# Multiplying the gates by the gelu straight out of PSUM in the dense expert loop

## The chip, the core and the metric

The kernel is one program on one core of a Trainium2 chip. It has five engines that run their own instruction streams in order: TensorE (PE, matrix products, results into PSUM banks), VectorE (DVE), ScalarE (ACT), GpSimd (POOL) and SyncE (SP, which here only issues transfers). The metric is the device time of one execution in microseconds. Three runs of the kernel before took 5031.38, 5035.41 and 5036.19 us; the median is 5035.41 us.

## The reference, cut to what matters

One layer of a hybrid backbone for 256 context tokens and 1024 sample tokens. The part that counts here is the last stage, PEER: 16384 experts of one neuron each, of which every token uses 16 in each of 8 heads.

```
idx  = top-16 experts of each head      # 128 of 16384 for a token
g    = softmax(scores of those)
act  = gelu(x . u_tab[idx])             # first layer
out  = sum over idx of (g * act) * v_tab[idx]   # second layer
```

The product `g * act` is what the change touches. A layer norm follows. Output: both token groups and the final states of a recurrence that runs earlier.

## The kernel before, in words

Two methods compute PEER side by side. The first 640 sample tokens (5 blocks of 128, `DB = 5`) go through all 16384 experts as dense matrix products, with a gate of zero where a token does not use an expert. The other 3 sample blocks and the context tokens are *gathered*: for each of a token's 128 experts a row of `u`, and later of `v`, is fetched by an indirect transfer issued on POOL, and DVE multiplies and adds it up, one instruction of 128x1024 for each row (`experts`, lines 1063 for `u` and 1072 for `v`). The vectors `h` and `y` of that sum live in PSUM, in a pool `pg` of one buffer.

The dense loop (`dense`, line 1133) runs over 32 steps `c` of 4 chunks of 128 experts each, `n = 4c + e`. For a chunk, `weighted(n)` gives the weights W, 128 experts x 640 tokens: gates `gt` (loaded from `d_GD`, two chunks to a tile) times the gelu of the first layer. For 72 of the 128 chunks (`EARLY`) the gelu was computed in an earlier stage and is loaded back from `d_AD` into a tile `a`; for the other 56 `first_layer` computes it here: two halves of 320 tokens, each 24 matmuls into one PSUM bank, which ACT turns into `a` by a gelu (line 1122). DVE multiplies `gt` by `a` (line 1160, 128x640). Then ACT copies W to `wh`, and DVE or POOL subtracts to get the rest `wl` (lines 205 and 206: every product is done as three products of rounded parts, so the tables `u` and `v` are split into `uh`, `ul`, `vh`, `vl` in the same way). The second layer multiplies W of the previous step by the table `v`: token block 0 adds up in two banks (`sums`) over the whole loop; blocks 1 to 4 take two banks each in every step, which DVE adds to `acc` (line 1146).

The dense loop's banks come from two pools of two buffers (`pa`, `pb`), taken in turn, so a product can begin when the bank of four products earlier is free. Before the change a first-layer bank is free after its gelu, a second-layer bank after its addition on DVE.

The order on each engine is made by a scheduler at build time, from its own model of times; gathered rows, dense additions and splits are mixed on DVE in that fixed order. A wait of one instruction holds up all behind it on that engine. At the end of a gathered block, `finish` (lines 1022 to 1035) norms and stores it, and the next block's `h` is loaded (line 1057) when the stored tile's buffer is free.

Of the kernel before, what the change touches and what calls it, by code (L numbers as in the profile page):

```python
# [11 lines left out]
F32 = mybir.dt.float32  # L12
# [4 lines left out]
AF = mybir.ActivationFunctionType  # L17
ALU = mybir.AluOpType
AX = mybir.AxisListType

P = 128
# [15 lines left out]
DB = 5  # L37
# [13 lines left out]
HALF = DB * P // 2  # L51
WSHARE = 0.5
GT = 64
# [48 lines left out]
def body(ctx, tc, A, O):  # L102
    nc = tc.nc
# [46 lines left out]
    def bank(s, banks=None):  # L150
        n = count["bank"] = count["bank"] + 1
        banks = banks or s.banks
        return banks[n % len(banks)].tile([P, 512], F32, tag="bank", name=f"bank{n}")

    def mm(out, terms, first=True, last=True):
        ops = []
        for l, r in terms:
            if len(l) == 1:
                ops.append((l[0], r[0]))
            else:  # L160
                ops += [(l[0], r[0]), (l[0], r[1]), (l[1], r[0])]
        for i, (l, r) in enumerate(ops):
            nc.tensor.matmul(out, l, r, start=(first and i == 0), stop=(last and i == len(ops) - 1))  # L163
# [33 lines left out]
    def elt(share):  # L197

        count["lo"] += 1
        n = count["lo"]  # L200
        return nc.gpsimd if int(n * share) != int((n - 1) * share) else nc.vector

    def split_into(hi, lo, src, eng):

        nc.scalar.activation(hi, src, AF.Copy)  # L205
        note(eng, eng.tensor_tensor(lo, src, hi.bitcast(F32), op=ALU.subtract))  # L206
# [14 lines left out]
    def sub(op, *idx):  # L221
        return tuple(o[idx] for o in op)
# [690 lines left out]
    def new_T(pool, s, nb):  # L913
        if s.native:
            return (pool.tile([P, KT, nb * P], F32, name="hT"),)
        return (pool.tile([P, KT, nb * P], F32R, name="hTh"), pool.tile([P, KT, nb * P], F32R, name="hTl"))
# [91 lines left out]
    def final_vectors(s, new):  # L1008
        vec = []
        for src in (mod_d[s.c:s.c + 1, 5 * D:6 * D], A["ln2_g"], A["ln2_b"]):  # L1010
            t = new()
            nc.sync.dma_start(t[:], src.to_broadcast([P, D]))
            vec.append(t)
        return vec
# [11 lines left out]
    def second_norm(s, b, y, out, pool, vec, eng):  # L1026
        rows = slice(b * P, (b + 1) * P)
        st = pool.tile([P, 2, 6], F32, tag="st", name="st", bufs=2)
        for i in range(2):
            nc.vector.bn_stats(st[:, i, :], y[:, i * 512:(i + 1) * 512])  # L1030
        sc, of = statistics(pool, st[:], EPS)
        nc.scalar.activation(y[:], y[:], AF.Identity, scale=sc, bias=of)
        nc.vector.tensor_tensor(y[:], y[:], vec[1][:], op=ALU.mult)
        eng.tensor_tensor(y[:], y[:], vec[2][:], op=ALU.add)
        nc.sync.dma_start(out[rows, :], y[:])
# [72 lines left out]
    def table(pool, src, tag, bufs, raws, eng):  # L1108

        r = pool.tile([P, D], F32, tag="raw" + tag, name="raw", bufs=raws)  # L1110
        nc.sync.dma_start(r[:], src)
        return split(pool, r[:], [P, D], tag, bufs=bufs, eng=eng)

    def first_layer(s, T, n, pool, bufs, share):

        U = table(pool, A["peer_uT"][n].rearrange("p k e -> p (k e)"), "u", bufs, 2, elt(share))
        a = pool.tile([P, DB * P], F32, tag="a", name="a", bufs=2)
        for t0 in range(0, DB * P, HALF):
            ts = slice(t0, t0 + HALF)
            ps = bank(s)  # L1120
            mm(ps[:, :HALF], [(sub(U, ALL, slice(k * P, (k + 1) * P)), sub(T, ALL, k, ts)) for k in range(KT)])
            nc.scalar.activation(a[:, ts], ps[:, :HALF], AF.Gelu_apprx_tanh)
        return a

    def dense(s, T, GD, AD, pool, accs, out):

        def spare():
            count["spare"] += 1
            return pool.tile([P, D], F32, tag=("uh", "uh", "uh", "ul", "ul", "ul", "rawu", "rawu", "rawv", "rawv")[count["spare"]], name="spare", bufs=2 if count["spare"] > 5 else 3)

        def second_layer(c, W, V, b):
            for h in range(2):
                cs = slice(h * 512, (h + 1) * 512)
                kept = b == 0
                ps = sums[h] if kept else bank(s)
                mm(ps[:], [(sub(W[e], ALL, slice(b * P, (b + 1) * P)), sub(V[e], ALL, cs)) for e in range(4)], c == 0 or not kept, c == 31 or not kept)
                if kept and c < 31:
                    continue
                if c == 0:
                    nc.scalar.activation(accs[b][:, cs], ps[:], AF.Copy)  # L1140
                elif c == 31:
                    t = pool.tile([P, 512], F32, tag="a", name="t", bufs=2)
                    nc.vector.tensor_tensor(t[:], ps[:], vec[0][:, cs], op=ALU.mult)
                    nc.vector.tensor_tensor(accs[b][:, cs], accs[b][:, cs], t[:], op=ALU.add)
                else:
                    nc.vector.tensor_tensor(accs[b][:, cs], accs[b][:, cs], ps[:], op=ALU.add)  # L1146

        pair = {}

        def weighted(n):  # L1150
            if n % 2 == 0:
                pair[0] = pool.tile([P, DB * P // GT, 2, GT], F32, tag="gt", name="gt", bufs=2)
                nc.sync.dma_start(pair[0][:], GD[:, :, n:n + 2, :].rearrange("c p j t -> p c j t"))
            gt = pair[0][:, :, n % 2, :]
            if n in EARLY:
                a = pool.tile([P, DB * P], F32, tag="a", name="a", bufs=2)
                nc.sync.dma_start(a[:], AD[EARLY.index(n)])
            else:
                a = first_layer(s, T, n, pool, 3, 0.5)
            nc.vector.tensor_tensor(gt, a[:].rearrange("p (c t) -> p c t", t=GT), gt, op=ALU.mult)  # L1160
            hi, lo = (pool.tile([P, DB * P], F32R, tag="w" + i, name="w" + i, bufs=6) for i in "hl")
            split_into(*(t[:].rearrange("p (c t) -> p c t", t=GT) for t in (hi, lo)), gt, elt(WSHARE))
            return hi, lo

        sums = [pc.tile([P, 512], F32, tag="bank", name=f"sums{h}") for h in range(2)]
        last, todo = None, []
        for c in range(33):
            W, V = [], []
            if c == 32:
                vec = final_vectors(s, spare)  # L1170
                for b in range(DB):
                    x = spare()
                    nc.sync.dma_start(x[:], s.X1[b * P:(b + 1) * P, :])
                    if b == 0:
                        accs[b] = spare()
                        nc.scalar.activation(accs[b][:], x[:], AF.Copy, scale=ALPHA)
                        continue
                    (nc.gpsimd if TP else nc.vector).tensor_tensor(accs[b][:], accs[b][:], vec[0][:], op=ALU.mult)
                    nc.vector.scalar_tensor_tensor(accs[b][:], x[:], ALPHA, accs[b][:], op0=ALU.mult, op1=ALU.add)
            for e in range(4):  # L1180
                if c < 32:
                    W.append(weighted(4 * c + e))
                if e < 2:
                    for b in todo[:3]:
                        second_layer(c - 1, *last, b)
                    todo = todo[3:]
                if c < 32 and e > 0:
                    for i in ((0,), (1, 2), (3,))[e - 1]:
                        V.append(table(pool, A["peer_v"].rearrange("(i j) d -> j i d", j=NK)[4 * c + i], "v", 4, 2, elt(0.5)))
            last, todo = (W, V), list(range(DB))  # L1190
        x = spare()
        nc.sync.dma_start(x[:], s.X1[s.nt - P:, :])
        for b in range(DB):
            second_norm(s, b, accs[b], out, pool, vec, nc.gpsimd if b < TB else nc.vector)
        return vec, x
# [37 lines left out]
    with tpool(SP, "tp") as fp:  # L1233
        T = new_T(fp, SP, SP.tt)
# [236 lines left out]
```

## Time and profile before

| | us |
|---|---|
| profiled execution | 5048.65 |
| its span | 5046.9 |
| median of three runs | 5035.41 |
| dense loop on PE, from its first second-layer product | 3577 to 4885 |
| after the dense loop | 4885 to 5047 |

PE is busy 4327.6 us (86%), DVE 4040.6 (80%), POOL 3176.4 (63%), ACT 1901.8 (38%) of the span. These are averages over stages with different limits; only the last 1470 us run the code that is changed. An instruction's time in the trace goes on until its result is written, so two in a row overlap a little: from the start of one to the start of the next is less than the time shown for one. The granted clock of TensorE stands as a share of its full speed.

### The profile page before, as it was taken

To read this page: it belongs to the slowest core of one execution; us is meant where nothing else is said; L and a number is where in the kernel's file an instruction comes from. 1 tells how busy PE (TensorE), PEld (TensorE's weight loads), DVE (VectorE), ACT (ScalarE), POOL (GpSimd) and SP (SyncE) were. 2 spreads that over 40 slices of the span, in tenths; PEclk is the share of its full clock that TensorE was granted. 3 is DMA by queue.
4 is the path that set the end of the run, shared out by engine and by line. 5 is a ranking of instruction groups with operands and counts; after the bars stand their busy time and mean duration, and the time that the engine had idled before them with its cause. 6 is when DMAs were issued, how large, how long until landed. Compare 5 with 4: busy or idle time off the path is not lost.

```text
span 5046.9 us, 67691 instructions
## 1 busy us (share of the span) xinstructions
PE 4327.6 (86%) x23707; PEld 3762.1 (75%) x23707; DVE 4040.6 (80%) x6725; ACT 1901.8 (38%) x2795; POOL 3176.4 (63%) x2297
## 2 busy tenths in 40 slices
PE   6888798899999679879798888889799999999970
PEld 4666687777777669857677888889688888888860
DVE  6778664989995786566759899887688989988898
ACT  4546333336664112221433765555222222222210
POOL 1456442478887665467665577778566676766775
PEclk8999899999999889989899999999899999999985
DMA  6676656798889853388786477788988999989987
GB/s 209 222 233 202 184 175 203 247 326 301 299 303 341 296 189 124 96 322 299 263 275 212 147 267 289 256 290 301 332 313 317 342 328 345 330 307 342 314 316 300
DMA packets 601089, 1357.25 MB, mean 269 GB/s; under 512 B 63230, under 2 KB 283079, under 8 KB 595116
## 3 DMA queue, kind: packets, MB, share of 16 engines
q1 hardware_dynamic: 404908, 658.69, 39.0%
q0 software_dynamic: 187776, 680.61, 37.6%
q10 hardware_dynamic: 8064, 13.64, 0.7%
q8 instruction: 186, 3.05, 0.2%
q14 instruction: 155, 1.27, 0.1%
HBM read 1182.81 MB, written 169.93 MB: 268 GB/s over the span
## 4 chain that ended last, share of the span: by engine, by line
PE 21%; DVE 17%; issue 8%; DMA 7%; POOL 4%; ACT 1%; SPq 0%; POOLq 0%; ACTq 0%; DVEq 0%
PE bank L163 16%; PE bank L172 3%; DVE row L1063 3%; DVE y L1072 2%; POOL row L1050 2%; DMA row<-in_peer_v,idxQ 2%; DVE hot L1094 2%; PE sums L163 2%; DMA row<-in_peer_v,idxP 1%; DVE gt L1160 1%; DMA row<-in_peer_u,idxQ 1%; DVE half L968 1%; DVE terms L972 1%; DVE S L932 1%; PE bank L1101 1%
## 5 line engine op out<-in xcount | busy, mean ns | idle before, releaser
L1072 DVE SCALAR_TENSOR_TENSOR y<-row,act,y 128x1024 f32<-128x1024 f32 x635 | 816.2, 1285 | 179.2 <-DMA row<-in_peer_v,idxP 109.4
L1063 DVE SCALAR_TENSOR_TENSOR row<-row,h 128x1024 f32<-128x1024 f32 x640 | 763.8, 1213 | 129.3 <-DMA row<-in_peer_u,idxP 69.9
L163 PE MATMUL bank<-hTh,ul 128*128 128x320 f32 x2048 | 642.9, 317 | 25.4 <-POOL ul L206 25.1
L163 PE MATMUL bank<-hTh,uh 128*128 128x320 f32 x2048 | 645.4, 315 | 11.7 <-ACT uh L205 11.7
L163 PE MATMUL bank<-hTl,uh 128*128 128x320 f32 x2048 | 645.7, 316 | 0.0
L1050 POOL DMA_INDIRECT row<-in_peer_u,idxQ x384 | 421.3, 1097 | 264.4 <-DVE row L1063 161.7
L206 POOL TENSOR_TENSOR wl<-wr,wh 128x1024 fp32r<-128x1024 f32 x148 | 363.9, 2460 | 333.7 <-ACT wh L205 311.9
L1050 POOL DMA_INDIRECT row<-in_peer_v,idxQ x384 | 416.2, 1084 | 246.8 <-DVE y L1072 163.8
L163 PEld LDWEIGHTS bank<-hTh,ul 128*128 128x128 f32 x2048 | 391.0, 192 | 33.9 <-POOL ul L206 33.7
L163 PE MATMUL bank<-vh,wh 128*128 128x512 f32 x1024 | 397.5, 393 | 17.8 <-DVE acc L1146 16.3
L163 PEld LDWEIGHTS bank<-hTh,uh 128*128 128x128 f32 x2048 | 394.2, 192 | 14.3 <-ACT uh L205 13.0
L163 PE MATMUL bank<-vl,wh 128*128 128x512 f32 x1024 | 400.3, 392 | 0.0
L163 PE MATMUL bank<-vh,wl 128*128 128x512 f32 x1024 | 395.7, 391 | 0.0
L163 PEld LDWEIGHTS bank<-hTl,uh 128*128 128x128 f32 x2048 | 393.4, 192 | 1.2
L1050 POOL DMA_INDIRECT row<-in_peer_u,idxP x256 | 276.3, 1079 | 143.6 <-DVE row L1063 83.6
L205 ACT ACTIVATE wh<-wr 128x1024 fp32r<-128x1024 f32 x176 | 186.0, 1059 | 442.8 <-issue 192.7
L1050 POOL DMA_INDIRECT row<-in_peer_v,idxP x256 | 279.9, 1093 | 92.5 <-issue 36.7
L1095 POOL TENSOR_TENSOR oa<-hot,tr 128x512 f32<-128x512 bf16 x160 | 220.2, 1386 | 85.9 <-DVE hot L1094 59.1
L205 ACT ACTIVATE wh<-gt 128x640 fp32r<-128x640 f32 x128 | 94.5, 740 | 466.0 <-DVE gt L1160 384.2
L206 POOL TENSOR_TENSOR ul<-raw,uh 128x1024 fp32r<-128x1024 f32 x100 | 245.6, 2456 | 27.6 <-ACT uh L205 24.3
L1098 ACT ACTIVATE ob<-hot 128x512 f32<-128x512 bf16 x160 | 181.3, 1136 | 184.7 <-DVE hot L1094 169.6
L1101 PE MATMUL bank<-ob,oa 128*128 128x128 f32 x1280 | 188.7, 294 | 66.1 <-POOL oa L1095 51.1
(455 smaller groups left out, 12697.9 us busy)
## 6 DMA issues: line engine op xcount, KB each, us to landing
raw<-in_peer_uT SPq DMA_DIRECT2D x128, 512.0 KB
raw<-in_peer_v SPq DMA_DIRECT2D x128, 512.0 KB
wr<-in_w_in SPq DMA_DIRECT2D x112, 512.0 KB
d_GD<-G SPq DMA_DIRECT2D x40, 1024.0 KB
gt<-d_GD SPq DMA_DIRECT2D x64, 640.0 KB
w<-in_w_ada SPq DMA_DIRECT2D x48, 512.0 KB
wr<-in_w_query SPq DMA_DIRECT2D x48, 512.0 KB
d_AD<-a SPq DMA_DIRECT2D x72, 320.0 KB
```

What stands on the lines that cost most here:

```text
L163: nc.tensor.matmul(out, l, r, start=(first and i == 0), stop=(last and i == len(ops) - 1))
L172: nc.tensor.matmul(out, a, b, start=(i + j == 0), stop=(i == KT - 1 and j == len(ops) - 1))
L205: nc.scalar.activation(hi, src, AF.Copy)
L206: note(eng, eng.tensor_tensor(lo, src, hi.bitcast(F32), op=ALU.subtract))
L932: nc.vector.match_replace(S2[:], v[:, g, 0:8], Sg, NEG)
L1050: i = nc.gpsimd.indirect_dma_start(out=t[:], out_offset=None, in_=A[tab], in_offset=bass.IndirectOffsetOnAxis(ap=idx[:, k:k + 1], axis=0))
L1063: nc.vector.scalar_tensor_tensor(t[:], t[:], 1.0, h[:], op0=ALU.mult, op1=ALU.mult, accum_out=act[:, k:k + 1])
L1072: nc.vector.scalar_tensor_tensor(y[:], t[:], act[:, k:k + 1], y[:], op0=ALU.mult, op1=ALU.add)
L1094: nc.vector.tensor_tensor(hot[:].rearrange("p k t q -> p k (t q)"), keys8[:], key[:, None, t0:t0 + 4, :].rearrange("p o t q -> p o (t q)") ...
L1095: note(nc.gpsimd, nc.gpsimd.tensor_tensor(oa[:], hot[:, :, :, 0].rearrange("p k t -> p t k"), tr[:, 2, t0:t0 + 4, None].to_broadcast([P, 4 ...
L1098: nc.scalar.activation(ob[:], hot[:, :, :, 1].rearrange("p k t -> p t k"), AF.Copy)
L1101: nc.tensor.matmul(ps[:, i * P:(i + 1) * P], oa[:, i, :], ob[:, i, :], start=True, stop=True)
```

## The change

For the 56 chunks whose first layer runs in the dense loop, the gelu is written back into the PSUM bank that it reads, and DVE multiplies `gt` by it from there, half by half: two instructions of 128x320 with one operand in PSUM, in place of one of 128x640 with both in SBUF. The tile `a` is no longer used for these chunks, only for the 72 that are loaded. The early stage calls `first_layer` without gates and is as before.

```diff
-    def first_layer(s, T, n, pool, bufs, share):
+    def first_layer(s, T, n, pool, bufs, share, gt=None):
         U = table(pool, A["peer_uT"][n].rearrange("p k e -> p (k e)"), "u", bufs, 2, elt(share))
-        a = pool.tile([P, DB * P], F32, tag="a", name="a", bufs=2)
+        if gt is None:
+            a = pool.tile([P, DB * P], F32, tag="a", name="a", bufs=2)
         for t0 in range(0, DB * P, HALF):
             ...
-            nc.scalar.activation(a[:, ts], ps[:, :HALF], AF.Gelu_apprx_tanh)
-        return a
+            if gt is None:
+                nc.scalar.activation(a[:, ts], ps[:, :HALF], AF.Gelu_apprx_tanh)
+            else:
+                nc.scalar.activation(ps[:, :HALF], ps[:, :HALF], AF.Gelu_apprx_tanh)
+                part = gt[:, t0 // GT:(t0 + HALF) // GT, :]
+                nc.vector.tensor_tensor(part, ps[:, :HALF].rearrange("p (c t) -> p c t", t=GT), part, op=ALU.mult)
+        return None if gt is not None else a
...
                 nc.sync.dma_start(a[:], AD[EARLY.index(n)])
+                nc.vector.tensor_tensor(gt, a[:].rearrange("p (c t) -> p c t", t=GT), gt, op=ALU.mult)
             else:
-                a = first_layer(s, T, n, pool, 3, 0.5)
-            nc.vector.tensor_tensor(gt, a[:].rearrange("p (c t) -> p c t", t=GT), gt, op=ALU.mult)
+                first_layer(s, T, n, pool, 3, 0.5, gt)
```

The change also shifts the order that the scheduler makes. Line 1160 becomes 1164 (loaded chunks) and 1128 (the new halves), line 1146 becomes 1152.

On DVE, where the last gathered block begins (its `h` is about to be loaded), before; `bank_36291` to `bank_36333` are the banks of token blocks 1 and 2 of one step:

```order
L1033 TENSOR_TENSOR r<-r,row 128x1024
L1160 TENSOR_TENSOR gt<-a,gt 128x10x64
L206 TENSOR_TENSOR vl<-raw,vh 128x1024
L1160 TENSOR_TENSOR gt<-a,gt 128x10x64 x2
L206 TENSOR_TENSOR wl<-gt,wh 128x640 x2
L1146 TENSOR_TENSOR acc_29995<-acc_29995,bank_36291 128x512
L1146 TENSOR_TENSOR acc_29995<-acc_29995,bank_36305 128x512
L1063 SCALAR_TENSOR_TENSOR row,act<-row,h 128x1024 x4
L1146 TENSOR_TENSOR acc_29996<-acc_29996,bank_36319 128x512
L1146 TENSOR_TENSOR acc_29996<-acc_29996,bank_36333 128x512
```

And the same place after the change:

```order
L1033 TENSOR_TENSOR r<-r,row 128x1024
L1128 TENSOR_TENSOR gt<-bank_36221,gt 128x5x64
L206 TENSOR_TENSOR vl<-raw,vh 128x1024
L206 TENSOR_TENSOR wl<-gt,wh 128x640 x2
L1063 SCALAR_TENSOR_TENSOR row,act<-row,h 128x1024 x4
L1152 TENSOR_TENSOR acc_29995<-acc_29995,bank_36291 128x512
L1152 TENSOR_TENSOR acc_29995<-acc_29995,bank_36305 128x512
L1063 SCALAR_TENSOR_TENSOR row,act<-row,h 128x1024
L1152 TENSOR_TENSOR acc_29996<-acc_29996,bank_36319 128x512
L1152 TENSOR_TENSOR acc_29996<-acc_29996,bank_36333 128x512
```

The first four gathered rows of the new block have moved ahead of the two additions of token block 1.

On DVE at the end of the dense loop, before; `acc_29998` is the last token block's sum, and `y` the gathered block's:

```order
L1072 SCALAR_TENSOR_TENSOR y<-row,act,y 128x1024
L1033 TENSOR_TENSOR acc_29998<-acc_29998,spare 128x1024
L1072 SCALAR_TENSOR_TENSOR y<-row,act,y 128x1024
L1034 TENSOR_TENSOR acc_29998<-acc_29998,spare 128x1024
L1072 SCALAR_TENSOR_TENSOR y<-row,act,y 128x1024 x76
L1022 TENSOR_TENSOR r<-y,spare 128x1024
```

And after the change:

```order
L1072 SCALAR_TENSOR_TENSOR y<-row,act,y 128x1024
L1033 TENSOR_TENSOR acc_29998<-acc_29998,spare 128x1024
L1072 SCALAR_TENSOR_TENSOR y<-row,act,y 128x1024
L1034 TENSOR_TENSOR acc_29998<-acc_29998,spare 128x1024
L1072 SCALAR_TENSOR_TENSOR y<-row,act,y 128x1024 x71
L1022 TENSOR_TENSOR r<-y,spare 128x1024
```

76 gathered rows stand behind the last dense instruction before, and 71 now. Counted from the addition that reads the last dense bank, there are 86 before and 80 now.

## Rows read from the trace of the kernel before

**Rows 1.** Stages: window, length, busy time by engine, clock, DMA share, GB/s.
```profile
core 0: us, PE busy (x) PEld busy (x) DVE busy (x) ACT busy (x) POOL busy (x), PEclk, DMA share, GB/s
3577.00:4885.00 1308.00, 1278.66 (x6503) 1116.36 (x6504) 1136.10 (x1298) 333.85 (x443) 882.12 (x646) 0.99 0.92 326
4885.00:5047.00 162.00, 5.58 (x24) 4.27 (x24) 144.91 (x144) 8.49 (x12) 95.59 (x90) 0.53 0.81 301
```

**Rows 2.** Timeline of DVE at the end: start, length, instruction, count.
```profile
4958.97 74.16 DVE L1072 SCALAR_TENSOR_TENSOR y<-row,act,y 128x1024 f32<-128x1024 f32 x56 [0.33 <-DVE y L1072]
```

**Rows 3.** Waits in the dense loop: us in total, times, longest.
```profile
ACT wh L205 <- DVE gt L1160: 369.1, 96, 10.9
DVE acc L1146 <- PE bank L163: 53.5, 58, 2.9
PE bank L163 <- DVE acc L1146: 16.3, 6, 6.6
```

**Rows 4.** Groups in the dense loop: busy us, mean ns; idle before, releasers.
```profile
L1160 DVE TENSOR_TENSOR gt<-a,gt 128x640 f32<-128x640 f32 x126 | 169.6, 1347 | 30.2 <-issue 19.0 <-ACT a L1122 4.9 <-DMA a<-d_AD 3.6
L1146 DVE TENSOR_TENSOR acc<-acc,bank 128x512 f32<-128x512 f32 x240 | 160.2, 684 | 54.9 <-PE bank L163 53.5 <-issue 0.7
```

**Rows 5.** Two lines by source: shortest, median, longest in ns.
```profile
L1160 DVE TENSOR_TENSOR gt<-a,gt x126: 811/821/5840, 3594.2 to 4867.0; 128x640 f32<-128x640 f32 x126
L1146 DVE TENSOR_TENSOR acc<-acc,bank x240: 672/684/692, 3646.6 to 4849.1; 128x512 f32<-128x512 f32 x120
```

**Rows 6.** Timeline of POOL and DVE around single instructions.
```profile
4401.20 2.40 POOL L206 TENSOR_TENSOR ul<-raw,uh 128x1024 fp32r<-128x1024 f32 x1 [0.33 <-issue]
4401.54 2.75 DVE L1160 TENSOR_TENSOR gt<-a,gt 128x640 f32<-128x640 f32 x1 [0.55 <-ACT a L1122]
4038.59 0.82 DVE L1160 TENSOR_TENSOR gt<-a,gt 128x640 f32<-128x640 f32 x1
4039.33 1.21 DVE L1063 SCALAR_TENSOR_TENSOR row<-row,h 128x1024 f32<-128x1024 f32 x1
4138.02 2.48 DVE L1146 TENSOR_TENSOR acc<-acc,bank 128x512 f32<-128x512 f32 x4
```

**Rows 7.** Timeline of PE: the products that followed the larger gaps.
```profile
3779.35 0.80 PE L163 MATMUL bank<-vh,wh 128*128 128x512 f32 x1 [3.78 <-DVE acc L1146]
4138.76 0.50 PE L163 MATMUL bank<-vh,wh 128*128 128x512 f32 x1 [2.37 <-DVE acc L1146]
4416.50 0.50 PE L163 MATMUL sums<-vh,wh 128*128 128x512 f32 x1 [1.78 <-issue]
4472.55 0.80 PE L163 MATMUL bank<-vh,wh 128*128 128x512 f32 x1 [6.60 <-DVE acc L1146]
4747.73 0.50 PE L163 MATMUL sums<-vh,wh 128*128 128x512 f32 x1 [1.51 <-ACT wh L205]
```

**Rows 8.** Stages again: just behind the gap at 3779.
```profile
3780.00:3790.00 10.00, 10.00 (x36) 8.07 (x35) 3.20 (x5) 1.03 (x1) 0.78 (x1) 0.78 0.80 269
```

**Rows 9.** Timeline of DVE, ACT and PE ahead of two gaps.
```profile
3753.50 3.16 DVE L1160 TENSOR_TENSOR gt<-a,gt 128x640 f32<-128x640 f32 x1
4459.18 1.28 DVE L1146 TENSOR_TENSOR acc<-acc,bank 128x512 f32<-128x512 f32 x2 [0.78 <-PE bank L163]
4466.18 1.03 ACT L1059 ACTIVATE h<-hs 128x1024 f32<-128x1024 f32 x1 [8.42 <-DMA hs<-d_H2Q]
4467.24 1.22 DVE L1063 SCALAR_TENSOR_TENSOR row<-row,h 128x1024 f32<-128x1024 f32 x1 [6.78 <-ACT h L1059]
4465.33 0.39 PE L163 MATMUL bank<-vl,wh 128*128 128x512 f32 x1
4465.56 0.39 PE L163 MATMUL bank<-vh,wl 128*128 128x512 f32 x1
```

**Rows 10.** Timeline of ACT and DVE: one gelu and its multiplication.
```profile
4408.07 0.42 ACT L1122 ACTIVATE a<-bank 128x320 f32<-128x320 f32 x1
4419.92 2.00 DVE L1160 TENSOR_TENSOR gt<-a,gt 128x640 f32<-128x640 f32 x1
```

## The prediction

> **What bounds the kernel now.** I read the stages first. From 3577 to 4885 us PE is busy 1278.7 of 1308 us at a clock of 0.99, so the dense loop lasts as long as its matrix products and the 29 us in which PE waits; DVE is busy 1136.1 us there and the transfers are at 0.92 of their capacity [rows 1]. Then PE is done, and from 4885 to 5047 us DVE is busy 144.9 of 162 us [rows 1]. The timeline of that end shows why: 56 gathered rows in a row in 74.16 us, one every 1.324 us, with no waits between them [rows 2]. So the end of the kernel is the end of PE's loop plus the DVE work that the order has left behind it. The waits say how the two engines are tied inside the loop: DVE's additions wait for PE 58 times, 53.5 us in all, and PE waits for them 6 times, 16.3 us in all [rows 3]. DVE mostly walks at PE's heels with time to spare. Making DVE quicker in the loop is worth only what ends one of PE's waits, or what lets the order put more gathered rows before PE's end.
>
> **The multiplication itself.** The groups and the lines by source belong together. The old multiplication has a median of 821 ns, but a mean of 1347 and a longest of 5840 [rows 4, 5]. The addition that has one operand in PSUM runs 240 times between 672 and 692 ns, mean 684 [rows 4, 5]. The timeline shows where the difference comes from: a POOL subtraction ran from 4401.20 to 4403.60, the DVE multiplication began at 4401.54 and ended at 4404.29, 0.69 us after POOL's end, about the time it would take alone [rows 6]. With both operands in SBUF a DVE instruction stands still until POOL's is done; with one in PSUM it does not, in 240 cases out of 240. So the new halves should not be held up by POOL.
>
> Their cost by start-to-start steps: an undisturbed 640-wide multiplication takes 0.74 us (4038.59 to 4039.33), and four 512-wide additions from PSUM take 2.48 us, of which the last one's own 0.684, so 0.60 each [rows 4, 6]. The 128 columns between them make 0.14 us, hence a half of 320 columns 0.60 - 1.5 x 0.14 = 0.39 us. Per chunk 0.78 us in place of an undisturbed 0.74, or of 1.27 with the usual hold-up (1.347 less the 0.08 of overlap; the mean is over loaded and computed chunks alike). Over 56 chunks DVE is relieved of 71.1 - 43.7 = 27 us; the ends are 4 us (a half costs as much as a 512-wide addition) and 27.
>
> The Trainium skill, Perfetto Trace Analysis, section "Optimizing Scalar/DVE Operations", speaks against the change: it gives about 60 ns of fixed cost for a VectorE access to SBUF and about 125 for PSUM. By that, an estimate, two halves would cost 2 x 125 - 60 = 190 ns more than one whole, 10.6 us over 56 chunks, if no hold-up went away. The rows above show 0.04 us a chunk, 2.2 us, so the extra cost for PSUM is not in this trace's steps; by either, the relief stays.
>
> The gelu on ACT only changes its destination. ACT is busy 334 of 1308 us in the loop [rows 1], and the chain to `wh` waits for the multiplication, not for ACT (369.1 us) [rows 3], so I take nothing for it, in either direction. The second instruction of each pair can now run while PE still computes the other half, which shortens the wait for `wh` a little.
>
> **What the relief is worth, term by term.**
>
> *A, the end.* The order has 80 gathered rows behind the addition of the last dense bank, where there were 86. Six rows at 1.324 us are 7.9 us [rows 2]. The loop must then take in six more, some 8 us of DVE, which the 27 us pay for. I take -7.9; ends -5 (if rows arrive late, as some do just after 4885) and -8.
>
> *B, PE's waits that hung on a held-up multiplication.* Before the gap of 3.78 us at 3779 the multiplication at 3753.50 took 3.16 us in place of 0.8, and another just behind it 2 us, ahead of the additions that PE waited for [rows 7, 9]. After such a gap the clock is below full for a while: 0.78 over the next 10 us, another 2.2 us [rows 8]. I take 6.0 us for that one. The gaps of 1.78 and 1.51 us before `sums` hang on `wh`, and so on the multiplication; I take 3.3. The gap of 2.37 at 4138 followed held-up subtractions, which the change leaves as they are: nothing. B is -9.3; ends 0 and -20 (all of the 16.3 us and the 3.3).
>
> *C, the last gathered block's start.* At 4459 DVE made two additions of token block 1, then waited 6.78 us for `h`, whose load ACT had waited for 8.42 us, and PE stood still for 6.6 us until the additions of token block 2 [rows 7, 9]. In the new order the first four rows, which need `h`, stand ahead of the additions of token block 1. The load of `h` hangs on the store of the previous block, which a quicker multiplication hardly moves. So PE can compute two products of 12 matmuls fewer before it stands still; a matmul steps by 0.227 us [rows 9], 24 of them take 5.4. C is +5.4; ends 0 (if `h` comes that much earlier) and +8 (if the clock falls further).
>
> *D, banks held for longer.* A first-layer bank was free after its gelu, and is now free after DVE has come round to it. PE comes back to such a bank after three other products, and after the parts of `sums` it can do, at least 9 us by the step of 0.227 us. The trace has no such wait. From below it is 0: the same four banks are released by DVE's additions for most of the loop, with only 16.3 us of waits. From above there is one case: a gelu ended at 4408.5 and its multiplication at 4421.9, 13 us later [rows 10]. There held-up instructions stood ahead of it, most of which go away. I take +2, near the lower end, and 24 as the upper (1 us in each of the 24 steps with two chunks).
>
> The loaded tiles `a` now have their two buffers to themselves, so they come earlier; DVE waits 3.6 us for them in the loop [rows 4], and I count nothing.
>
> Sum: -7.9 - 9.3 + 5.4 + 2 = -9.8 us, from 5048.65 (span 5046.9) to 5038.9 for the profiled execution. The median of the runs is 13.2 us below the profiled one; I carry the difference over: 5035.4 - 9.8 = 5025.6, rounded to 5026.
>
> **Rivals.**
>
> *All of PE's waits on DVE go.* If relief shortens every DVE queue, and `h` comes earlier, then -7.9 - 16.3 - 3.3 = -27.5: 5008. For it: DVE is what PE waits for in almost all gaps [rows 7]. Against it: the subtractions are still held up by POOL, and the gap of 6.6 us hangs on a load.
>
> *Nothing comes of it.* DVE waits longer for PE and for rows (transfers at 0.92), and the rows saved at the end come back as waits for rows, since their 3.1 MB take 9.6 us at 326 GB/s [rows 1]: A is eaten, B and C cancel, 5035. For it: the spare time of DVE in the loop is already there and unused.
>
> *The banks are the new wait.* If DVE comes to the first-layer banks too late in each of the 24 steps with two chunks, PE waits about 1 us each time: +24, with A and C -7.9 + 5.4, so 5035.4 + 21.5 = 5057. It decides when the multiplication lags its gelu by more than the 9 us that PE takes to come round; one lag of 13 is there [rows 10]. The Trainium skill, PSUM — Partial Sum Buffer, section "Summary: rules for kernel authors", has this rule: evacuate promptly, PSUM is tight. That the trace bears it out nowhere, since no bank is held so here, is why it is not more than a rival.
>
> **How the numbers follow.** About 0.2%, 10 us, is what a measurement of this kernel can tell from no change. The forecast has 0.48: its own range is 5015 to 5038, so I put 0.20 of it faster by over 0.2%, 0.25 within and 0.03 slower. All waits gone: 0.20, faster. Nothing: 0.17, same. Banks: 0.15, slower. Together 0.40, 0.42 and 0.18. The range reaches into the two outer cases, 5009 to 5047.
>
> **What would show it.** A: 71 rows undisturbed at the end, and PE's last product to the end of the span about 154 us in place of 162. The multiplications of 320 columns all close to 0.48 us, none above 0.6; if they spread like the old ones, the first step is wrong. B: no gap near 3779. C: a gap near 4460 of about 12 us in place of 6.6, if I read the order rightly. D: PE waits with the new multiplication as releaser; more than 10 us of them in all, and the sign of the forecast is wrong. It would also be wrong if the loop on PE, 1308 us before, came out longer than 1314.

## The result: 5112 us, slower, outside the range

| | before | after |
|---|---|---|
| median of six runs, us | 5037.17 (5031.38 to 5062.69) | 5112.24 (5108.82 to 5123.57) |
| profiled execution's span | 5046.9 | 5109.6 |
| last product on PE | 4890.2 | 4961.8 |
| from there to the end of the span | 156.7 | 147.8 |

The ratio is 1.0149, interval [1.0134, 1.0163]: 75 us slower, where 10 us faster was forecast. The end behind PE is 8.9 us shorter, as forecast. All of the loss, and more, is in the dense loop: the two profiled spans are 62.7 us apart, 71.6 more up to the last product and 8.9 less behind it. (The profiled execution of before lay 11 us above the median, so the spans differ by less than the medians.) The stages show it, before and after, cut where PE's last product ends (columns as in [rows 1]). Before:

```profile
3577.00:4890.00 1313.00, 1283.66 (x6525) 1120.47 (x6526) 1141.10 (x1307) 334.05 (x444) 884.27 (x647) 0.99 0.92 325
4890.00:5047.00 157.00, 0.58 (x3) 0.16 (x1) 139.91 (x135) 8.29 (x11) 93.44 (x88) 0.51 0.82 304
```

After:

```profile
3577.00:4962.00 1385.00, 1304.73 (x6525) 1121.42 (x6523) 1098.83 (x1369) 326.93 (x444) 871.12 (x654) 0.99 0.88 309
4962.00:5110.00 148.00, 0.21 (x1) 0.00 (x0) 133.87 (x129) 8.27 (x11) 87.65 (x82) 0.52 0.81 301
```

The loop is 72 us longer for the same 6525 products. PE is idle in it for 80.3 us in place of 29.3, and busy for 21 us more. DVE is *less* busy, by 42.3 us, although six more instructions than the 56 added halves fall into the loop, and idle for 286 us in place of 172; so it has been relieved, and stands still instead. (The 27 us that were forecast are for the computed chunks alone. Line 1160 mixes them with the loaded ones, so the 42.3 cannot be set against the 27 piece by piece.) The waits of DVE in the loop say for what (us in total, times, longest). Before, the three rows that matter:

```profile
DVE acc L1146 <- PE bank L163: 53.5, 58, 2.9
DVE row L1063 <- DMA row<-in_peer_u,idxQ: 15.9, 13, 3.3
DVE gt L1160 <- DMA gt<-d_GD: 2.5, 1, 2.5
```

After:

```profile
DVE gt L1164 <- DMA gt<-d_GD: 140.0, 27, 9.1
DVE row L1063 <- DMA row<-in_peer_u,idxQ: 40.2, 32, 3.3
DVE acc L1152 <- PE bank L163: 15.7, 23, 2.0
```

The first row is new in size: the multiplication of the *loaded* chunks, which the change does not touch, stands still 27 times for its gates, 140 us in all. And the additions wait for PE much less than in [rows 3]: DVE has gone from walking behind PE to holding PE up. The groups that answer to [rows 4]:

```profile
L1164 DVE TENSOR_TENSOR gt<-a,gt 128x640 f32<-128x640 f32 x70 | 62.9, 925 | 152.1 <-DMA gt<-d_GD 140.0 <-issue 11.1 <-DMA a<-d_AD 1.0
L1128 DVE TENSOR_TENSOR gt<-bank,gt 128x320 f32<-128x320 f32 x112 | 53.9, 481 | 8.3 <-ACT bank L1126 8.1 <-issue 0.3
```

Lines 1128 and 1164 together are busy 116.8 us, where line 1160 was 169.6.

Where the new wait stands is seen in one step on the timelines. Before, DVE's multiplications and additions (gathered rows and splits between them are left out):

```profile
4018.59 0.69 DVE L1146 TENSOR_TENSOR acc<-acc,bank 128x512 f32<-128x512 f32 x1 [0.37 <-PE bank L163]
4019.19 0.82 DVE L1160 TENSOR_TENSOR gt<-a,gt 128x640 f32<-128x640 f32 x1
...
4029.63 0.69 DVE L1146 TENSOR_TENSOR acc<-acc,bank 128x512 f32<-128x512 f32 x1
...
4038.59 0.82 DVE L1160 TENSOR_TENSOR gt<-a,gt 128x640 f32<-128x640 f32 x1
...
4046.11 3.32 DVE L1160 TENSOR_TENSOR gt<-a,gt 128x640 f32<-128x640 f32 x1
```

After, POOL's split that frees the first gate tile, and DVE from there to the end of the stall:

```profile
4023.53 1.58 POOL L206 TENSOR_TENSOR wl<-gt,wh 128x640 fp32r<-128x640 f32 x1 [0.44 <-ACT wh L205]
...
4030.73 1.34 DVE L1152 TENSOR_TENSOR acc<-acc,bank 128x512 f32<-128x512 f32 x2
...
4034.78 0.68 DVE L1152 TENSOR_TENSOR acc<-acc,bank 128x512 f32<-128x512 f32 x1
4042.03 1.56 DVE L1164 TENSOR_TENSOR gt<-a,gt 128x640 f32<-128x640 f32 x2 [6.57 <-DMA gt<-d_GD]
...
4044.65 0.68 DVE L1152 TENSOR_TENSOR acc<-acc,bank 128x512 f32<-128x512 f32 x1
```

And SP's queue over the same time, after:

```profile
4025.14 3.48 SPq L1159 DMA_DIRECT2D gt<-d_GD  x2
4042.89 1.07 SPq L1163 DMA_DIRECT2D a<-d_AD  x2
4051.39 1.43 SPq L1111 DMA_DIRECT2D raw<-in_peer_v  x2
```

Before, the four multiplications of a step are spread out, one or two of them far behind the additions. After, the two loaded ones stand side by side with additions before and behind them. The load of their gates is issued at 4025.14, when POOL's split has freed the tile at 4025.11 (there are two gate tiles), and the multiplications begin at 4042.03, 16.9 us later. The order on each engine is fixed at build time, so this place could be read ahead of any run: the pair amid the additions, and on SP the gates side by side just ahead. The forecast speaks only of two other places.

So, theory 1: with the computed chunks out of it, the ring of two tiles `a` (two buffers, taken in turn) no longer makes a loaded chunk wait for the computed chunks of the step before. The loads of `a` move a step ahead, the scheduler puts the multiplications that use them earlier, ahead of their gates, and DVE, in order, stands still with the additions and splits behind it. Rival 1: the multiplication out of PSUM itself, by the banks it holds, and the stall is only a symptom.

### The profile page after: what moved, and what is told of

The parts are those of the page before. It is cut to its first block, busy times and chain, and to the rows that moved or that the text cites. A ratio compares the mean times of both kernels' runs of the same rounds, so it can differ in the third digit from the quotient of the medians.

```text
span 5109.6 us, 67792 instructions
## 1 busy us (share of the span) xinstructions
PE 4344.4 (85%) x23707; PEld 3754.5 (73%) x23707; DVE 3988.4 (78%) x6781; ACT 1892.6 (37%) x2795; POOL 3158.2 (62%) x2297
## 4 chain that ended last, share of the span: by engine, by line
DVE 17%; issue 13%; PE 12%; DMA 9%; POOL 7%; ACT 1%; SPq 0%; POOLq 0%; ACTq 0%; DVEq 0%
PE bank L163 7%; POOL row L1050 4%; PE bank L172 3%; DVE row L1063 3%; DVE y L1072 3%; DMA gt<-d_GD 2%; DMA row<-in_peer_v,idxQ 2%; DVE hot L1094 2%; POOL wl L206 1%; DMA row<-in_peer_u,idxQ 1%; DMA row<-in_peer_v,idxP 1%; DVE terms L972 1%; POOL ul L206 1%; PE bank L1101 1%; DVE S L932 1%
## 5 line engine op out<-in xcount | busy, mean ns | idle before, releaser
L205 ACT ACTIVATE vh<-raw 128x1024 fp32r<-128x1024 f32 x128 | 131.7, 1053 | 541.0 <-PE bank L163 219.0
```

## The experiments

| run | median us | ratio to before | interval | DVE's wait for gates, us |
|---|---|---|---|---|
| after | 5112.24 | 1.0149 | 1.0134 to 1.0163 | 140.0 |
| e1 ring kept | 5036.37 | 0.9991 | 0.9977 to 1.0005 | 3.1 |
| e2 gelu in `wh` | 5134.45 | 1.0177 | 1.0153 to 1.0201 | 131.6 |
| e3 loaded late | 5034.93 | 0.9988 | 0.9976 to 1.0000 | none shown |
| e4 one loaded tile | 5106.86 | 1.0131 | 1.0105 to 1.0157 | 99.9 |
| e5 `v` ahead of `a` | 5177.36 | 1.0257 | 1.0232 to 1.0282 | 169.5 |
| e6 `a` behind `v` | 5049.44 | 1.0013 | 1.0002 to 1.0023 | 4.2 |
| e7 before, loaded late | 5047.09 | 1.0013 | 1.0001 to 1.0025 | none shown |
| e8 e3 with e6 | 5042.46 | 1.0004 | 0.9993 to 1.0015 | none shown |
| e9 after, 4 row buffers | 5302.12 | 1.0515 | 1.0498 to 1.0533 | 158.2 |
| e10 e9 and 3 gate tiles | 5206.10 | 1.0327 | 1.0303 to 1.0352 | 18.2 |
| e11 before, 4 row buffers | 5209.67 | 1.0330 | 1.0312 to 1.0347 | 6.9 |
| e12 e3 again | 5037.03 | 0.9993 | 0.9982 to 1.0004 | none shown |

Ratios are to runs of the kernel before on the same chip, medians 5037.17 (after), 5042.52 (e1 to e4), 5037.16 (e5 to e8) and 5041.61 us (e9 to e12).

**e1: the change, with the ring kept.**

```diff
-        if gt is None:
-            a = pool.tile([P, DB * P], F32, tag="a", name="a", bufs=2)
+        a = pool.tile([P, DB * P], F32, tag="a", name="a", bufs=2)
+        if gt is not None:
+            nc.scalar.activation(a[:, :1], ident[:, :1], AF.Copy, scale=0.0, bias=1.0)
...
-                nc.vector.tensor_tensor(part, ps..., part, op=ALU.mult)
+                nc.vector.scalar_tensor_tensor(part, ps..., a[:, :1], part, op0=ALU.mult, op1=ALU.mult)
```

> The changed kernel, gelu and multiplication in PSUM as changed, but a computed chunk again takes a tile of the ring `a`: ACT writes 1.0 into its first column, and the multiplication reads that column as a factor (x 1.0). Theory 1 (the two loaded multiplications of a step have moved ahead of their gates on DVE, because the ring of `a` no longer ties them to the computed chunks): the order of DVE is again that of before, DVE's wait for gt<-d_GD falls from 140 us to under 15, the time is 5015 to 5045. Rival 1 (banks held longer, and products out of PSUM): the banks are held as in the changed kernel, so the time stays at 5100 to 5120.

It measured 5036.37. The waits of the loop show both sides:

```profile
DVE acc L1153 <- PE bank L163: 66.0, 63, 4.2
PE bank L163 <- DVE acc L1153: 13.1, 4, 4.4
DVE gt L1165 <- DMA gt<-d_GD: 3.1, 2, 2.6
```

Gelu and multiplication stay in PSUM, banks are held as in the changed kernel, and the loss is gone. The additions walk behind PE again. Rival 1 falls.

**e2: the ring left, without PSUM.** This is the other half of the same question: the kernel before with only the ring split.

```diff
...
+            hi, lo = (pool.tile(... tag="w" + i, name="w" + i, bufs=6) for i in "hl")
...
-                a = first_layer(s, T, n, pool, 3, 0.5)
-            nc.vector.tensor_tensor(gt, a[:].rearrange(...), gt, op=ALU.mult)
-            hi, lo = (pool.tile(... tag="w" + i, name="w" + i, bufs=6) for i in "hl")
+                a = first_layer(s, T, n, pool, 3, 0.5, hi)
+            nc.vector.tensor_tensor(gt, (a[:] if n in EARLY else hi[:].bitcast(F32)).rearrange(...), gt, op=ALU.mult)
```

> The kernel before, with nothing in PSUM: the gelu of a computed chunk is written to SBUF, into the chunk's own tile `wh` (rounded there as that tile's type asks, so the gelu is less exact), and one multiplication of 128x640 reads it there; the bank is free after the gelu as before. Only the loaded chunks use the ring `a`. Theory 1: DVE's order has the two loaded multiplications side by side amid the additions as in the changed kernel, so 100 us or more of waits for gt<-d_GD and a time of 5085 to 5125. Rival 1: no bank is held and nothing is read from PSUM, so 5025 to 5045.

It measured 5134.45, 9 us over the range of theory 1. The groups:

```profile
L1162 DVE TENSOR_TENSOR gt<-wh,gt 128x640 f32<-128x640 f32 x56 | 74.4, 1329 | 9.4 <-ACT wh L1123 8.8 <-issue 0.6
L1162 DVE TENSOR_TENSOR gt<-a,gt 128x640 f32<-128x640 f32 x70 | 62.0, 913 | 138.8 <-DMA gt<-d_GD 131.6 <-issue 7.2
```

No product comes out of PSUM, and the stall is there. The mean of the first row, 1329 ns, is of the size of the hold-up beside POOL that [rows 4 to 6] speak of, where two halves from PSUM take 2 x 481 less their overlap. So e1 and e2 separate the two things that the change does: the ring makes the loss, PSUM does not.

**e3: the changed kernel, with the loaded multiplications held back on DVE.**

```diff
+                for b in todo:
+                    second_layer(c - 1, *last, b)
+                todo = []
                 if c < 32:
                     W.append(weighted(4 * c + e))
-                if e < 2:
-                    for b in todo[:3]:
-                        second_layer(c - 1, *last, b)
-                    todo = todo[3:]
...
-                    nc.vector.tensor_tensor(accs[b][:, cs], accs[b][:, cs], ps[:], op=ALU.add)
+                    done[0] = nc.vector.tensor_tensor(accs[b][:, cs], accs[b][:, cs], ps[:], op=ALU.add)
...
-                nc.vector.tensor_tensor(gt, a[:].rearrange(...), gt, op=ALU.mult)
+                behind(nc.vector.tensor_tensor(gt, a[:].rearrange(...), gt, op=ALU.mult), done[0])
```

> The changed kernel, with the loaded multiplications ordered behind the last addition of the step, on DVE (second-layer calls of a step written ahead of its chunks, and an order-only dependence). Banks and PSUM as changed. Theory 1: the gates have had some 15 us more to land, the waits for gt<-d_GD fall under 40 us and stand behind the additions, so PE does not wait for them: 5010 to 5050, the best case a little below before. Rival 1: 5100 to 5120.

It measured 5034.93, in the range of theory 1. The timeline of DVE (additions and loaded multiplications of one step) shows the pair behind the last addition, without a wait:

```profile
4053.67 0.69 DVE L1152 TENSOR_TENSOR acc<-acc,bank 128x512 f32<-128x512 f32 x1 [0.73 <-PE bank L163]
4056.55 0.68 DVE L1152 TENSOR_TENSOR acc<-acc,bank 128x512 f32<-128x512 f32 x1
4057.16 2.21 DVE L1165 TENSOR_TENSOR gt<-a,gt 128x640 f32<-128x640 f32 x2
```

**e4: one tile for loaded chunks.** `bufs=1` in place of 2 for the loaded `a` (and for the tile `t` that shares its tag).

> The changed kernel with one buffer in place of two for the loaded tiles `a`: the second loaded multiplication of a step moves behind the additions, the first stays amid them. Theory 1: the first still stands ahead of its gates in most steps, the second no longer: a part of the loss comes back, waits for gt<-d_GD of 40 to 120 us, 5050 to 5100. Rival 1: 5100 to 5120, since banks are as changed; a later load of `a` could make it worse.

It measured 5106.86, 0.2% less than the changed kernel, with intervals that overlap, and just above the range of theory 1. The wait for gates came down from 140 to 99.9 us, the median by 5 us. So the loss does not go in step with this wait. In the order only the second of the two multiplications had moved behind the additions. One multiplication ahead of its gates is nearly as bad here as two side by side. Its time lies in rival 1's range, so this run by itself speaks for neither.

**e5: is it DVE's stall, or SP's?** In the step above SP also stands still. It issues the next `a` only when the stalled multiplications have freed it, and the `v` tables behind come later; ACT waits 124.3 us for them in the loop, before 14.1. SP itself waits 386.8 us for line 1164 to free `a`, and waited 153.2 us for line 1160 before. e5 has `a` behind the step's second `v` load on SP (`second[0]`) and leaves the pair amid the additions on DVE.

```diff
...
-                nc.sync.dma_start(a[:], AD[EARLY.index(n)])
+                behind(nc.sync.dma_start(a[:], AD[EARLY.index(n)]), second[0])
```

> The changed kernel, in which on SP alone the loads of the loaded tiles `a` are ordered behind the loads of the step's first two `v` tables. The two loaded multiplications keep their place amid the additions on DVE; what goes is that SP, waiting for those multiplications to free `a`, holds up the `v` loads behind it. Theory 1a (the loss is DVE's own standing still for gt<-d_GD): waits for gt<-d_GD stay at 80 us or more, 5080 to 5120. Theory 1b (the loss comes by SP: the `v` tables come late, and ACT waits 124 us for them): ACT's wait for raw<-in_peer_v falls under 60 us, 5030 to 5060. In between, both.

It measured 5177.36, above both ranges. The waits of the loop:

```profile
ACT vh L205 <- DMA raw<-in_peer_v: 230.8, 52, 11.3
DVE gt L1168 <- DMA gt<-d_GD: 169.5, 31, 10.0
```

And what SP waited for there:

```profile
SPq L1111 <- DVE vl L206: 336.3, 60, 25.9
SPq L1111 <- POOL vl L206: 322.3, 44, 23.9
SPq L1167 <- DVE gt L1168: 147.7, 16, 16.5
```

ACT's wait was to fall and nearly doubled. On SP the wait for `a` did fall, from 386.8 to 147.7 us, but the `v` loads then waited for the splits that free their raw tiles, 336.3 and 322.3 us where the changed kernel has 201.6 and 181.7. So this run made the waits of DVE and ACT both longer, and by itself does not part 1a from 1b. e6 says more.

**e6: `a` behind the last `v` load of the step before.** The edit is that of e5 with the last `v` load. On DVE it puts the loaded multiplications among the first-layer halves.

> The changed kernel, with the loads of the loaded tiles `a` ordered on SP behind the last `v` load of the step before. On DVE this puts the loaded multiplications among the first-layer halves, behind the additions, one by one. Theory 1: waits for gt<-d_GD under 30 us, 5015 to 5045. The rival of held banks: 5100 to 5120.

It measured 5049.44, 0.13% above before and a little above the range.

```profile
ACT vh L205 <- DMA raw<-in_peer_v: 98.7, 55, 11.8
DVE gt L1168 <- DMA gt<-d_GD: 4.2, 3, 1.7
```

ACT waits 98.7 us for `v` tables, and PE's last product still comes at 4887.5, before at 4890.2. Late `v` tables of that amount cost no more than e6 loses as a whole, 0.13% with an interval up to 0.23%. What e6 lacks, and the changed kernel, e2, e4, e5 and e9 have, is DVE's wait for gates. That is against 1b; what late `v` tables cost in the changed kernel's own order, beside the stall, is not shown.

**e7 and e8: what PSUM is worth in one order, and whether `v` still costs.** e7 is the kernel before with the edit of e3; e8 is e3 with the edit of e6.

> The kernel before (gelu and one 128x640 multiplication in SBUF), with the edit of the third run: loaded multiplications ordered behind the last addition of the step. Against the third run (5034.9) it prices the product out of PSUM in one and the same order. By the terms of the forecast PSUM is worth some 10 us, so 5035 to 5050 here; if PSUM is worth nothing, 5030 to 5040; if held banks cost, this is the faster of the two, 5015 to 5030.

> The third run's kernel and the sixth's together: loaded multiplications behind the last addition on DVE, and the loads of `a` behind the last `v` load on SP. If what was left of ACT's waits for `v` in the third run (54 us) still costs PE anything, this is faster than the third run, 5015 to 5032; if not, the same, 5030 to 5040.

e7 measured 1.0013 (5047.09 us, in its first range), e3 0.9988 and 0.9993 (e12), each against the kernel before on its own chip. The quotient of e3 and e7 is 0.9975, from two sets of runs with an uncertainty of about 0.0017 (both intervals together): PSUM saves 12.6 us, give or take 9, in this order; with e12 it is 10 us. That is the size the forecast had for the relief, but it is got against an order that is 0.13% worse for the SBUF version, not against the kernel before. e8 measured 1.0004 (5042.46 us, above both its ranges), not faster than e3. But its edit did not shorten ACT's wait for `v`: 65.6 us, where e3 has 54.0. So whether anything is left to gain from `v` stays open.

**e9 to e11: the same bad order, with the gates there in time.** A third gate tile needs room, so all three have four buffers for gathered rows in place of five. e10 adds one edit to e9:

```diff
-                pair[0] = pool.tile([P, DB * P // GT, 2, GT], F32, tag="gt", name="gt", bufs=2)
+                pair[0] = pool.tile([P, DB * P // GT, 2, GT], F32, tag="gt", name="gt", bufs=3)
```

> A control for the next run: the changed kernel with four in place of five buffers for gathered rows, which makes room in SBUF. The loaded multiplications stand amid the additions as in the changed kernel. Both theories: DVE's waits for gt<-d_GD 100 to 180 us; 5100 to 5150, the rows coming somewhat later.

> The changed kernel with four buffers for rows and three in place of two for the gate tiles `gt`. The loaded multiplications stand amid the additions still, two or three additions earlier even; but a gate tile need not wait for the split that frees the tile two before it, so it can be loaded earlier. Theory 1 (the gates come too late for this order): waits for gt<-d_GD fall under 40 us and the time to within 25 us of the kernel before with four row buffers. A rival, that this place in the order is bad as such (the additions come later, whatever the gates do), or held banks: the time stays within 20 us of the control, 5090 to 5150.

> The second control: the kernel before with four buffers for gathered rows. Both theories: 5035 to 5065, waits for gt<-d_GD under 15 us.

All three are much slower than was expected of them, for fewer row buffers cost 3.3% by themselves (e11); that is told below. Against one another they answer: 5302.12 us for the changed kernel (e9), 5206.10 with a third gate tile (e10), 5209.67 for the kernel before (e11). The loop's waits in e9 and in e10:

```profile
DVE gt L1164 <- DMA gt<-d_GD: 158.2, 31, 8.6
PE sums L163 <- ACT wh L205: 62.3, 24, 5.1
PE bank L163 <- DVE acc L1152: 33.5, 17, 4.0
```

```profile
PE bank L163 <- DVE acc L1152: 19.9, 9, 4.3
PE sums L163 <- ACT wh L205: 18.7, 13, 4.0
DVE gt L1164 <- DMA gt<-d_GD: 18.2, 15, 2.9
```

In e10 the two multiplications still stand amid the additions: in most steps behind two of the eight, where e9 has three and the changed kernel five. With gates that land in time that place costs nothing: 96 us come back, where the loss was 92 (e9 less e11). So it is not the place as such, nor the banks, but the place ahead of its gates. (With the stall went what hangs on it: SP's wait for `a` fell from 377.6 to 154.3 us, ACT's for `v` from 224.0 to 155.6. So e10 does not part 1a from 1b either.)

**e12: does e3 beat the kernel before?**

> The third run's kernel once more, in more rounds, for whether it beats the kernel before: by the terms of the forecast (a relief of some 10 us once the loaded multiplications no longer wait for gates) 5025 to 5037, a ratio of 0.997 to 0.9995; if its first ratio of 0.9988 was chance, 1.000 or above.

It measured 5037.03, ratio 0.9993, interval to 1.0004. By their ratios both runs of e3 lie 4 to 6 us below before, and neither interval leaves 1; taken together, an estimate, they make 0.9991 give or take 0.0008. e3 is the best version found; that it beats the kernel before is not shown beyond doubt.

## Why the prediction was wrong, point by point

**The step that failed** reads: "The loaded tiles `a` now have their two buffers to themselves, so they come earlier; DVE waits 3.6 us for them in the loop [rows 4], and I count nothing." The first half is right. But an operand that comes earlier lets the scheduler place its reader earlier, and the reader has a second operand. I looked at the wait that goes, for `a` (3.6 us before, 1.0 after), put it at nothing, and did not ask for the operand that is late next, `gt`: 2.5 us before, 140.0 after. e1 to e3 and e9 to e11 show that the loss comes with this wait and goes with it; e4 shows that it is not in proportion to it. The loop, which the prediction's last sign wanted at no more than 1314 us, took 1385.

**How 140 us of DVE become 72 us of loop.** DVE had slack. In the sum over the loop its idle time rose by 114 us and its busy time fell by 42, which makes the 72. The waits for gates rose by 137.5 and those for rows of `u` by 24.3, while those for PE fell by 37.8. PE then waits for copies, splits and additions that come late. The three largest of its waits in the loop, after:

```profile
PE sums L163 <- ACT wh L205: 20.9, 13, 4.4
PE sums L163 <- POOL vl L206: 19.6, 12, 3.5
PE bank L163 <- DVE acc L1152: 19.1, 11, 7.6
```

Before, the same three were 3.6, 1.7 and 16.3 us. The additions are the smaller part of the rise; most of it stands before `sums`. A split on POOL is not in DVE's order, so it comes late by another path, such as late `v` tables or POOL's own waits for row buffers that DVE has yet to free. How the loss divides over these paths is not shown. Of the 72 us, 51 are PE's idle time and 21 longer products. After a gap the granted clock is below full for a while [rows 8], but this explains little of the 21: it is 0.99 in both stretches, and stood at its lower level, 1.2 GHz, for 30 us of the loop before and for 38 after by the trace's clock record, which makes some 4 us, an estimate. The other 17 are not explained.

**The multiplication itself: right.** By source, after:

```profile
L1128 DVE TENSOR_TENSOR gt<-bank,gt x112: 473/481/493, 3584.4 to 4937.6; 128x320 f32<-128x320 f32 x112
```

All 112 lie between 473 and 493 ns, so none is held up by POOL. The timelines of POOL and DVE show one with a POOL subtraction running across it, and behind it a split with both operands in SBUF, which takes 1.87 us. The step from the half to the next instruction was forecast at 0.39 us and is 0.40:

```profile
4016.19 1.58 POOL L206 TENSOR_TENSOR wl<-gt,wh 128x640 fp32r<-128x640 f32 x1
4016.59 0.49 DVE L1128 TENSOR_TENSOR gt<-bank,gt 128x320 f32<-128x320 f32 x1
4016.99 1.87 DVE L206 TENSOR_TENSOR vl<-raw,vh 128x1024 fp32r<-128x1024 f32 x1
```

Two halves thus cost 0.80 us against 0.74 for the whole. The Trainium skill, Perfetto Trace Analysis, section "Optimizing Scalar/DVE Operations", would have 0.19 more for the two accesses to PSUM, an estimate from its figures; the trace of the changed kernel shows 0.06. One slip of the prediction: it is the first half of a pair, not the second, that can run while PE computes the other.

**The gelu on ACT: right.** 112 of them took 47.0 us, a mean of 420 ns, against 428 before.

**A, the end: right.** -8.9 us, forecast -7.9. (The 162 us that the prediction names for this stretch count from 4885, when 24 products were still to come; from the last product it was 156.7, and is 147.8.) The sign of 71 undisturbed rows did not come true: 59 came in a row, as DVE's timeline shows, and those just ahead of them waited for their row, under 1 us each.

```profile
5017.73 78.14 DVE L1072 SCALAR_TENSOR_TENSOR y<-row,act,y 128x1024 f32<-128x1024 f32 x59 [0.74 <-DMA row<-in_peer_v,idxQ]
```

**B, waits that hung on held-up multiplications:** the gap at 3779 is gone as forecast; the largest near it is 1.84 us, at 3767. What it was worth cannot be read from this kernel, in which new gaps cover it. The forecast also left out that in the trace of before a split on DVE took 6.13 us at 3758.74, between the two multiplications that it names.

**C, the start of the last gathered block:** the order was read rightly, the size was not. Rows go first, and PE stands still until the additions. DVE's timeline:

```profile
4506.89 1.22 DVE L1063 SCALAR_TENSOR_TENSOR row<-row,h 128x1024 f32<-128x1024 f32 x1 [7.91 <-ACT h L1059]
4511.46 1.28 DVE L1152 TENSOR_TENSOR acc<-acc,bank 128x512 f32<-128x512 f32 x2
```

On PE, behind them:

```profile
4512.19 0.79 PE L163 MATMUL bank<-vh,wh 128*128 128x512 f32 x1 [7.64 <-DVE acc L1152]
```

The gap is 7.64 us where it was 6.60 [rows 7]: +1.0, forecast +5.4. I had PE stop two products sooner against an unmoved `h`; but the block's start is 40 us later, and PE and DVE stand differently to each other there; why the gap grew so little is not shown.

**D, banks held for longer: right.** PE waits once, 2.6 us, for the new multiplication; the forecast was 2. The rival that gave this as the price of a slower kernel had the sign and the wrong mechanism: at 24 us it could not have made 75.

**The rival "nothing comes of it" (5035)** is where the change goes once the stall is taken out: e1 0.9991, e3 0.9988 and 0.9993, e6 1.0013, e8 1.0004. DVE's busy time in the loop is 1116 us in e3 and 1133 in e1, 1141 before, for about the same number of gathered rows, and the time moves by about 0.1% either way.

## What to carry to other kernels

A tile ring is also a fence: whoever takes half of its users out frees the other half to be scheduled earlier, and has to price the wait for the *other* operands of what moves, not only the one that came sooner. On an engine in order, a multiplication ahead of its load is paid by all that stands behind it; hold it back by a dependence that only fixes the order (e3), or give its late operand one more buffer (e10). The Trainium skill, Trainium Kernel Development and Optimization, section "Best Practices", advises double-buffering, so that transfers overlap compute; here two gate tiles were too few for this order, with 158.2 us of waits (e9), and three were enough, with 18.2 (e10).

## What the runs showed that I had not expected

Five row buffers or four makes more difference than anything else tried: the kernel before went from 5041.61 to 5209.67 us with four (e11), ratio 1.0330 [1.0312, 1.0347]. In the whole span DVE's idle time ahead of the gathered multiplications and additions rose from 129.3 and 179.2 us to 231.7 and 274.3, nearly all of it waits for rows. Its groups, kernel before and then e11:

```profile
L1072 DVE SCALAR_TENSOR_TENSOR y<-row,act,y 128x1024 f32<-128x1024 f32 x635 | 816.2, 1285 | 179.2 <-DMA row<-in_peer_v,idxP 109.4 <-DMA row<-in_peer_v,idxQ 56.9 <-issue 2.3
```

```profile
L1072 DVE SCALAR_TENSOR_TENSOR y<-row,act,y 128x1024 f32<-128x1024 f32 x635 | 816.0, 1285 | 274.3 <-DMA row<-in_peer_v,idxP 150.1 <-DMA row<-in_peer_v,idxQ 109.7 <-issue 4.8
```

The loss is not the dense loop's alone: the first `sums` product comes 82 us later than before, some 45 us are lost from there to PE's last product and 44 behind it.

So with four buffers fewer transfers of rows are hidden behind DVE's work, and a tile added elsewhere at the price of a row buffer costs 168 us here, more than twice the stall of this case. Whether a sixth would gain was not tried.
